# A Silu one place later and two block-sum steps one stage earlier in a two-layer encoder kernel

## The chip, the cores and the metric

The kernel runs on one core of a Trainium2 chip. A core has a matrix engine (TensorE, in the profile PE, with its weight loads as PEld), three engines for elementwise work (VectorE: DVE, ScalarE: ACT, GpSimd: POOL), and queues that start DMA transfers (SP and POOL here). Each engine works through its own instruction queue in order and waits on semaphores for the others. The metric is the device time of one execution in microseconds.

## What is computed

The reference is an encoder of two layers over 512 tokens of width 1024. Both layers end in the same kind of channel mixer, and that is where the change lies:

```python
def conv_ffn(h, w_up, conv_w, conv_b, w_down):
    u, g = jnp.split(h @ w_up, 2, axis=-1)
    g = causal_dwconv(g, conv_w, conv_b)
    return (jax.nn.silu(g) * u) @ w_down
...
x = x + jnp.concatenate([mix_out, mem_out], axis=-1) @ w_out
x = x + conv_ffn(rmsnorm(x, norm_ffn_g[l]), ffn_w_up[l], ffn_conv_w[l], ffn_conv_b[l], ffn_w_down[l])
```

`w_up` has 2 x 2816 columns (up and gate), the convolution runs over three tokens, and `w_down` leads back to 1024. Ahead of the mixer the first layer has a matrix-memory head and a memory attention, the second a banded attention and a memory attention, each with an output projection (`w_out`). All is float32.

## The kernel before

Everything is held transposed: 128 channels on the partitions, 512 tokens along a row. A float32 factor is split into a high and a low part, and each product is three matmuls (high x high, high x low, low x high; `mm3`, lines 194 to 198). The split of a tile is a cast on ACT for the high part and a subtraction on DVE for the low part (`split`, lines 142 and 143).

**Out projection** (`OutProjection.finish`, line 710). For each of the eight x tiles it adds the projection to the residual on DVE (line 715), writes the tile to `xspill` through POOL's queue (716), squares it on ACT and adds the square on DVE for the norm (`Norm.add`, lines 284 to 291), and scales it by the gain into a high part on ACT and a low part on DVE (`scaled`, lines 331 and 332): these are the activations of the mixer. In the first layer it takes, behind x tiles 4, 5 and 6, one step each of `block_sums`.

**Block sums** (`block_sums`, line 781). Step k takes x tiles k and k + 4: two scaled copies on ACT (787), four subtractions of half tiles on DVE (796), and the split of the four results (four casts on ACT, four subtractions on DVE). It has four steps and they are a generator: whoever calls `next` on it has one step emitted at that place.

**Plain tiles** (`plain`, line 759). The mixer has 22 tiles of 128 hidden channels. The first three (PLAIN = 3) are computed plainly: gate and up projection of 24 matmuls each, the gate times the norm's row (770), the convolution's first product on ACT (750) and two taps on DVE (743), Silu on ACT (774), times the row (775), times up (778), split. The norm's row itself is made inside plain tile 0 (`Norm.finish`, line 293): a split of the sum of squares, two matmuls with ones (301), then Ln, Exp and Square on ACT and three products on DVE. The block-sum steps that are still left are woven into the plain tiles, one for each eight products. In the second layer all four steps are left: two fall into plain tile 1, two into plain tile 2.

**Later tiles** (`later` and `step`, lines 850 and 874). The other 19 tiles use a scheme that multiplies blocks of 256 tokens with seven products in place of eight; it needs sums of weight blocks (class `Forms`) and the block sums. One step computes one tile: on TensorE the chain on r1 (889 to 891: product, then ACT's copy to `up`), the chain on r2 (893; added on DVE in 894), the third chain, again on r1 (895; copied by ACT in line 882), the fourth on r3 (897), the fifth on r1 (900; copied by 882), products of the down projection with hidden tiles that are done (904, 911), a sixth on r1 (910), a seventh on r3 (912). r1 is one PSUM bank: its next chain can't start before the last copy out of it is done. The down products go through `add` (line 820): a copy on ACT (822) into a `bias` tile and an accumulating DMA through POOL (823).

What follows the products of a tile, its **tail** (class `Tail`), runs in the next tile's step: the last block's add (989), times the norm's row (992, 995), first tap on ACT (750), two taps on DVE (743), Silu on ACT (1007), the gate product on DVE (1010) and the split of the hidden tile. The weight sums and splits of the tile after it (`nxt`) run in the same step.

**What sets the order.** In `later` all instructions of TensorE, ACT and DVE stand in the order in which `step` emits them (`manual_schedule`, line 862). Outside of it a planner orders each engine's queue at compile time: it takes, of what is ready by its own estimate of costs, what comes first in the program. Tiles of one tag (`u` for splits, `t` for temporaries, `bias`) share a fixed number of buffers, and PSUM has three `mm`, three `sc` and two `tr` banks.

Of the kernel before, what the change touches and what calls it, by code (L numbers as in the profile page):

```python
# [19 lines left out]
KT = D // P  # L20
# [23 lines left out]
LOADS = [(0, 2, 0, 4), (0, 2, 4, 8)]  # L44
LOADS += [(2, 4, 2 * i, 2 * i + 2) for i in range(4)]
LOADS += [(4 * g, 4 * g + 4, 2 * i, 2 * i + 2) for g in (1, 2, 3) for i in range(4)]
UNITS = {3 + i: tuple((i, j) for j in range(*LOADS[i][2:])) for i in range(len(LOADS))}

H = S // 2
# [7 lines left out]
def trunk(  # L57
# [34 lines left out]
    def sb(tag, shape, dtype=F32):  # L92
        count[0] += 1
        return pool.tile(shape, dtype, tag=tag, name=f"{tag}{count[0]}", bufs=bufs[tag])

    def ps(tag):
        count[0] += 1
        return psum.tile([P, S], F32, tag=tag, name=f"p{tag}{count[0]}", bufs=pbufs[tag])
# [101 lines left out]
    def project(w, c0, act, tag="mm"):  # L200


        n = len(act)
        wh, wl = weights(rows(w, c0, P), n, P)
        o = ps(tag)
        for k in range(n):
            mm3(o, wh[:, k, :], wl[:, k, :], act[k][0], act[k][1], k == 0, k == n - 1)
            yield
        return o

    def run(gen):
        while True:
            try:
                next(gen)
            except StopIteration as end:
                return end.value
# [57 lines left out]
    def logarithms():  # L274

        pin(A.preload_act_table_set("natural_log_exp_and_others"))

    class Norm:
# [14 lines left out]
        def finish(self):  # L293


            parts = [sb("t", [P, S], F32R) for _ in range(2)]
            split(*parts, self.acc)
            yield 7.4
            o = ps("sc")
            for i, part in enumerate(parts):  # L300
                nc.tensor.matmul(o, onesr, part, start=i == 0, stop=i == 1)
            v, r, t = sb("rb", [P, S]), sb("t", [P, S]), sb("t", [P, S])
            A.activation(t, o, AF.Ln, scale=1.0 / D, bias=eps)
            V.tensor_scalar(v, o, 1.0 / D, EPS, op0=ALU.mult, op1=ALU.add)
            A.activation(r, t, AF.Exp, scale=-0.5)
            A.activation(t, r, AF.Square)
            yield 4
            V.scalar_tensor_tensor(t, t, -0.5, v, op0=ALU.mult, op1=ALU.mult)
            self.row = sb("rb", [P, S])
            V.scalar_tensor_tensor(self.row, t, 1.5, r, op0=ALU.add, op1=ALU.mult)  # L310
# [18 lines left out]
    def scaled(t, g):  # L329
        hi, lo = sb("u", [P, S], F32R), sb("u", [P, S], F32R)  # L330
        A.activation(hi, t, AF.Copy, scale=g)
        V.scalar_tensor_tensor(lo, t, g, f(hi), op0=ALU.mult, op1=ALU.subtract)  # L332
        return hi, lo
# [131 lines left out]
    with tc.manual_schedule(engines={mybir.EngineType.PE, mybir.EngineType.Activation, mybir.EngineType.DVE}):  # L465
# [20 lines left out]
        def step(products, os_, k, order):  # L486
            for a, b in order:
                for i, o in enumerate(os_):
                    c = slice(i * P, (i + 1) * P)
                    st, mv = kv[k][a], memT[k][b]  # L490
                    first, last = (k, (a, b)) == (0, order[0]), (k, (a, b)) == (KT - 1, order[-1])
                    if products == "keys":
                        nc.tensor.matmul(o, st[:, c], mv, start=first, stop=last)
                    else:
                        nc.tensor.matmul(o, mv[:, c], st[:, MEM:], start=first, stop=last)
# [194 lines left out]
    class OutProjection:  # L690
# [6 lines left out]
        def part(self, g, *ks):  # L697
            j0, j1, tag = self.groups[g]
            if j0 not in self.o:
                self.o.update((j, ps(tag)) for j in range(j0, j1))  # L700
            cols = slice(j0 * P, j1 * P)
            wh, wl = weights([self.w[k * P : (k + 1) * P, cols] for k in ks], len(ks), (j1 - j0) * P)
            for i, k in enumerate(ks):
                self.n[g] += 1
                for j in range(j0, j1):
                    c = slice((j - j0) * P, (j - j0 + 1) * P)
                    mm3(self.o[j], wh[:, i, c], wl[:, i, c], *self.mixes[k], self.n[g] == 1, self.n[g] == KT)
                    yield

        def finish(self, mixer):  # L710
            logarithms()
            norm = mixer.norm
            for j in range(KT):
                o = self.o[j] if j in self.o else run(project(self.w, j * P, self.mixes))
                V.tensor_add(xT[j], xT[j], o)
                pin(G.dma_start(xspill[j], xT[j]))
                norm.add(xT[j])
                mixer.act.append(scaled(xT[j], mixer.gain[:, j : j + 1]))
                if mixer.l == 0 and KT // 2 <= j < KT - 1:
                    next(mixer.forms)  # L720

    class ChannelMixer:
# [127 lines left out]
        def later(self):  # L850


            prep, tail = Forms(self, PLAIN), None
            prep.split_up()
            prep.sums()
            prep.split_second()
            prep.sum_third()
            prep.split_sums()
            prep.sum_fourth()
            prep.split_down()  # L860
            prep.split_gate()
            with tc.manual_schedule(
                engines={mybir.EngineType.PE, mybir.EngineType.Activation, mybir.EngineType.DVE}
            ):
                for j in range(PLAIN, FT):
                    self.beside()
                    tail, prep = self.step(j, prep, Forms(self, j + 1) if j + 1 < FT else None, tail)
            for part in (
                tail.last_block, tail.scaled, tail.first_tap, tail.scaled_up,
                tail.second_tap, tail.third_tap, tail.gated, tail.split,  # L870
            ):
                part()

        def step(self, j, w, nxt, tail):
            def then(o, *names):
                for name in names if o is not None else ():
                    getattr(o, name)()

            def sum_products(o, r, w, i):

                self.products(r, w, self.t(i))
                A.copy(o, r[:, :H])  # L882

            new = Tail(self, j)
            then(tail, "last_block", "scaled")
            w.split_fourth()
            then(tail, "scaled_up")
            r1, r2, new.r3 = ps("mm"), ps("mm"), ps("sc")
            new.up, new.u3, new.pre = sb("t", [P, S]), sb("t", [P, S]), sb("t", [P, S])
            self.products(r1, w.a11, self.b(0, 0), True)  # L890
            A.copy(new.up[:, :H], r1[:, :H])  # L891
            then(tail, "first_tap", "second_tap", "third_tap")
            self.products(r2, w.a12, self.b(1, 0), True)
            V.tensor_tensor(out=new.up[:, :H], in0=new.up[:, :H], in1=r2[:, :H], op=ALU.add)
            sum_products(new.up[:, H:], r1, w.s2, 2)
            then(nxt, "sums")
            self.products(new.r3, w.s1, self.t(1), True)
            then(tail, "gated")
            then(nxt, "split_second", "sum_third")
            sum_products(new.u3[:, :H], r1, w.s3, 3)  # L900
            then(tail, "split")
            then(nxt, "split_up")
            V.tensor_tensor(out=new.pre[:, H:], in0=new.u3[:, :H], in1=new.r3[:, :H], op=ALU.add)
            w.down_products(0, 2)
            then(nxt, "split_sums", "sum_fourth")
            w.add_down(0)
            then(nxt, "split_gate")
            w.add_down(1)
            then(nxt, "split_down")
            sum_products(new.pre[:, :H], r1, w.a22, 4)  # L910
            w.down_products(2, 4)
            self.products(new.r3, w.s4, self.b(1, 1))
            w.add_down(2)
            w.add_down(3)
            return new, nxt

    class Forms:


        def __init__(self, mixer, j):  # L920
            self.mixer = mixer
            self.units = UNITS.get(j, ())
            self.up, self.gate = mixer.load_pair(j)
# [57 lines left out]
    class Tail:  # L981
# [22 lines left out]

        def third_tap(self):
            next(self.taps)
            A.activation(self.acc, self.acc, AF.Silu)

        def gated(self):
# [313 lines left out]
    mixer = ChannelMixer(0, col["gffn"][:, 0:8], more_rows)  # L1323
# [138 lines left out]
    mixer = ChannelMixer(1, col["gffn"][:, 8:16], lambda: None)  # L1462
# [125 lines left out]
```

## Time and profile before

| What | Value |
|---|---|
| median of 3 runs | 1193.42 us (1190.77 to 1195.13) |
| the profiled execution | 1192.76 us |
| its span, first to last instruction | 1191.0 us |
| mean granted clock of TensorE | 0.996 |
| busy: PE, DVE, ACT, POOL | 1171.5, 986.8, 743.1, 143.0 us |
| channel mixer steps, layer 0 and layer 1 (first to last tail Silu) | 329.6 to 585.5 us, 893.2 to 1151.2 us |

A row of the profile's groups names the line, engine and operation, the tile written and those read, the shapes and the count; behind the bar stand busy time, mean duration in ns, and idle time of the engine just before, with what ended it. A row of the timeline gives start, duration, engine, line, operation, tiles, and in brackets idle time before it and what ended it. A row of the waits gives who waited for whom: total us, times, longest. A matmul's duration covers its way through the array, and matmuls overlap: their pitch is the distance of their starts.

### The profile page before, as it was taken

To read this page: it belongs to the slowest core of one execution; us is meant where nothing else is said; L and a number is where in the kernel's file an instruction comes from. 1 tells how busy PE (TensorE), PEld (TensorE's weight loads), DVE (VectorE), ACT (ScalarE), POOL (GpSimd) and SP (SyncE) were. 2 spreads that over 40 slices of the span, in tenths; PEclk is the share of its full clock that TensorE was granted. 3 is DMA by queue.
4 is the path that set the end of the run, shared out by engine and by line. 5 is a ranking of instruction groups with operands and counts; after the bars stand their busy time and mean duration, and the time that the engine had idled before them with its cause. 6 is when DMAs were issued, how large, how long until landed. Compare 5 with 4: busy or idle time off the path is not lost.

```text
span 1191.0 us, 19097 instructions
## 1 busy us (share of the span) xinstructions
PE 1171.5 (98%) x7149; PEld 1040.0 (87%) x7149; DVE 986.8 (83%) x1768; ACT 743.1 (62%) x1345; POOL 143.0 (12%) x238
## 2 busy tenths in 40 slices
PE   9999999999999999999999999999989999999997
PEld 9988888887899999999888888778878999999986
DVE  6776788789889988888788888987878998888865
ACT  6548677657566655555666666776755665555545
POOL 1211101010122111111020001101011111111100
PEclk9999999999999999999999999999989999999999
DMA  8645325244578766665662323236256766666551
GB/s 278 223 110 146 78 54 150 84 145 114 130 166 193 178 165 165 142 141 116 180 212 81 87 70 108 82 113 203 86 121 114 167 143 142 142 141 143 124 159 72
DMA packets 200623, 162.87 MB, mean 137 GB/s; under 512 B 8680, under 2 KB 176334, under 8 KB 200530
## 3 DMA queue, kind: packets, MB, share of 16 engines
q1 hardware_dynamic: 182066, 119.74, 34.3%
q0 software_dynamic: 17888, 40.86, 18.2%
q8 instruction: 56, 0.92, 0.3%
q10 hardware_dynamic: 576, 1.05, 0.2%
q14 instruction: 37, 0.30, 0.1%
HBM read 128.89 MB, written 36.66 MB: 139 GB/s over the span
## 4 chain that ended last, share of the span: by engine, by line
PE 74%; issue 14%; DVE 7%; ACT 3%; POOL 1%; DMA 1%; POOLq 0%; ACTq 0%; DVEq 0%
PE pmm L196 15%; PE pmm L197 14%; PE pmm L198 14%; PE ptr L197 5%; PE ptr L198 5%; PE ptr L196 5%; PE psc L198 3%; PE psc L196 3%; PE psc L197 3%; PE psc L602 2%; DVE wl L143 1%; DVE t L743 1%; ACT wh L142 1%; DVE fl L143 1%; PE ptr L1410 1%
## 5 line engine op out<-in xcount | busy, mean ns | idle before, releaser
L196 PE MATMUL pmm<-u,wh 128*128 128x512 f32 (+1 forms) x984 | 335.8, 342 | 2.9 <-ACT t L882 2.0
L197 PE MATMUL pmm<-u,wh 128*128 128x512 f32 (+1 forms) x984 | 331.9, 337 | 0.2 <-DVE u L332 0.2
L198 PE MATMUL pmm<-u,wl 128*128 128x512 f32 (+1 forms) x984 | 332.0, 338 | 0.0
L143 DVE TENSOR_TENSOR wl<-wr,wh 128x1024 fp32r<-128x1024 f32 (+4 forms) x172 | 195.6, 1138 | 81.8 <-ACT wh L142 81.4
L142 ACT CAST wh<-wr 128x1024 fp32r<-128x1024 f32 (+4 forms) x172 | 168.3, 981 | 81.9 <-PE pmm L197 31.6
L196 PEld LDWEIGHTS pmm<-u,wh 128*128 128x128 f32 x984 | 185.2, 188 | 22.1 <-ACT t L882 4.9
L198 PEld LDWEIGHTS pmm<-u,wl 128*128 128x128 f32 x984 | 185.0, 188 | 19.7 <-DVE wl L143 0.3
L197 PEld LDWEIGHTS pmm<-u,wh 128*128 128x128 f32 x984 | 185.2, 188 | 17.3 <-DVE u L332 0.5
L823 POOL DMA_DIRECT2D xspill<-bias x80 | 69.4, 884 | 428.9 <-ACT bias L822 402.9
L196 PE MATMUL ptr<-u,wh 128*128 128x512 f32 x272 | 106.4, 391 | 0.0
L197 PE MATMUL ptr<-u,wh 128*128 128x512 f32 x272 | 106.3, 391 | 0.0
L198 PE MATMUL ptr<-u,wl 128*128 128x512 f32 x272 | 105.9, 389 | 0.0
L196 PE MATMUL pmm<-u,fh 128*128 128x256 f32 x304 | 85.2, 280 | 6.3 <-ACT t L891 6.3
L142 ACT CAST fh<-pt 128x512 fp32r<-128x512 f32 x114 | 71.2, 625 | 27.2 <-DVE pt L940 26.5
L143 DVE TENSOR_TENSOR fl<-pt,fh 128x512 fp32r<-128x512 f32 x114 | 78.3, 688 | 8.4 <-ACT fh L142 5.5
L197 PE MATMUL pmm<-u,fh 128*128 128x256 f32 x304 | 84.7, 279 | 0.0
L198 PE MATMUL pmm<-u,fl 128*128 128x256 f32 x304 | 84.6, 278 | 0.0
L743 DVE SCALAR_TENSOR_TENSOR t<-t,cols,t 128x511 f32<-128x511 f32 x88 | 66.0, 750 | 10.4 <-ACT t L750 9.0
L822 ACT COPY bias<-ptr 128x512 f32<-128x512 f32 x80 | 46.9, 589 | 39.9 <-PE ptr L198 35.5
L196 PE MATMUL psc<-u,wh 128*128 128x256 f32 (+1 forms) x216 | 67.9, 314 | 0.3 <-ACT wh L142 0.3
L198 PE MATMUL psc<-u,wl 128*128 128x256 f32 (+1 forms) x216 | 67.6, 313 | 0.4 <-DVE wl L143 0.4
L197 PE MATMUL psc<-u,wh 128*128 128x256 f32 (+1 forms) x216 | 67.5, 313 | 0.0
(348 smaller groups left out, 2584.4 us busy)
## 6 DMA issues: line engine op xcount, KB each, us to landing
wr<-in_ffn_w_up_dram SPq DMA_DIRECT2D x50, 512.0 KB, 7.2
xspill<-bias POOLq DMA_DIRECT2D x80, 256.0 KB, 5.7
pt<-in_ffn_w_up_dram SPq DMA_DIRECT2D x38, 512.0 KB, 7.9
wr<-in_ffn_w_down_dram SPq DMA_DIRECT2D x34, 512.0 KB, 5.3
wr<-in_a_w_in_dram SPq DMA_DIRECT2D x20, 512.0 KB, 3.9
wr<-in_w_kv_dram SPq DMA_DIRECT2D x12, 512.0 KB, 4.0
xspill<-fh POOLq DMA_DIRECT2D x16, 256.0 KB, 2.6
xspill<-fl POOLq DMA_DIRECT2D x16, 256.0 KB, 2.7
```

What stands on the lines that cost most here:

```text
L142: high = A.copy(hi, src) if on_act else V.tensor_copy(hi, src)
L143: low = V.tensor_tensor(out=lo, in0=src, in1=f(hi), op=ALU.subtract)
L196: nc.tensor.matmul(o, lh, rh, start=first, stop=False, skip_group_check=more)
L197: nc.tensor.matmul(o, lh, rl, start=False, stop=False, skip_group_check=more)
L198: nc.tensor.matmul(o, ll, rh, start=False, stop=last, skip_group_check=more)
L602: nc.tensor.matmul(o, a, b, start=first and i == 0, stop=i == 1)
L743: V.scalar_tensor_tensor(acc[:, n:], src[:, : S - n], self.fw[:, c * FT + j : c * FT + j + 1], acc[:, n:], op0=ALU.mult, op1=ALU.add,)
L822: A.copy(t, o)
L823: G.dma_start(xspill[j], t, accum_op=ALU.add)
L1410: nc.tensor.transpose(tp[:, b * P : (b + 1) * P], es[T, h][:, b * P : (b + 1) * P], ident)
```

## The change

Two edits. The tail's Silu becomes a part of its own, and `step` calls it behind the third chain's copy instead of right behind the second tap on DVE. A table EARLY says behind which x tile how many block-sum steps are taken: in the first layer one each behind tiles 4, 5 and 7 (before: 4, 5, 6), in the second two behind tile 7 (before: none). The number of plain tiles, three, is the same before and after.

```diff
+EARLY = ({4: 1, 5: 1, 7: 1}, {7: 2})
...
                 pin(G.dma_start(xspill[j], xT[j]))
                 norm.add(xT[j])
                 mixer.act.append(scaled(xT[j], mixer.gain[:, j : j + 1]))
-                if mixer.l == 0 and KT // 2 <= j < KT - 1:
+                for _ in range(EARLY[mixer.l].get(j, 0)):
                     next(mixer.forms)
...
                 tail.last_block, tail.scaled, tail.first_tap, tail.scaled_up,
-                tail.second_tap, tail.third_tap, tail.gated, tail.split,
+                tail.second_tap, tail.third_tap, tail.silu, tail.gated, tail.split,
...
             self.products(r2, w.a12, self.b(1, 0), True)
             V.tensor_tensor(out=new.up[:, :H], in0=new.up[:, :H], in1=r2[:, :H], op=ALU.add)
             sum_products(new.up[:, H:], r1, w.s2, 2)
+            then(tail, "silu")
             then(nxt, "sums")
             self.products(new.r3, w.s1, self.t(1), True)
             then(tail, "gated")
...
         def third_tap(self):
             next(self.taps)
+
+        def silu(self):
             A.activation(self.acc, self.acc, AF.Silu)
```

## Prediction

> **What bounds the kernel now.** I read the page first, then the waits of the matmul engine's weight loads, then the timeline around the longest of those waits, and last the windows of single stages.
>
> ```profile
> span 1191.0 us, 19097 instructions
> PE 1171.5 (98%) x7149; PEld 1040.0 (87%) x7149; DVE 986.8 (83%) x1768; ACT 743.1 (62%) x1345; POOL 143.0 (12%) x238
> PEclk9999999999999999999999999999989999999999
> ```
>
> TensorE is busy for 98% of the span, so only what makes TensorE wait, or slows its clock, can be won. The clock row has one digit that is not 9, slice 29 (863 to 893 us): in one place TensorE ran slower. The execution took 1192.76 us, 1.8 us more than its span; the three timed runs have a median of 1193.42.
>
> ```profile
> PEld pmm L196 <- ACT t L891: 6.9, 3, 4.5
> PEld pmm L196 <- ACT t L882: 5.6, 13, 0.9
> L196 PEld LDWEIGHTS pmm<-u,wh 128*128 128x128 f32 x984 | 185.2, 188 | 22.1 <-ACT t L882 4.9 <-ACT u L142 1.0
> L196 PEld LDWEIGHTS pmm<-u,fh 128*128 128x128 f32 x304 | 57.6, 189 | 9.0 <-ACT t L891 6.9 <-ACT t L882 0.7
> ```
>
> These are the waits on the two copies out of r1's PSUM bank: L891, after a step's first chain, and L882, after its third to fifth. Both concern the steps of the later tiles, and both edits aim at them. Of the thirteen waits on L882 two (0.7 us, the `fh` group) belong to the last step of each layer and are not touched; the other eleven, 4.9 us, are fifth chains waiting for the third chain's copy.
>
> **Edit 1, the Silu.** One short step of layer 0 shows the cause (ACT, PE and DVE rows of the timeline):
>
> ```profile
> 357.42 0.63 ACT L1007 ACTIVATE t<-t 128x512 f32<-128x512 f32 x1 [1.89 <-DVE t L743]
> 357.95 0.35 ACT L882 COPY t<-pmm 128x256 f32<-128x256 f32 x1
> 356.60 0.28 PE L198 MATMUL pmm<-u,fl 128*128 128x256 f32 x1
> 357.96 0.28 PE L198 MATMUL psc<-u,wl 128*128 128x256 f32 x1
> 358.36 0.38 PE L196 MATMUL pmm<-u,wh 128*128 128x256 f32 x1
> 358.90 0.69 DVE L1010 TENSOR_TENSOR t<-t,t 128x512 f32<-128x512 f32 x1
> ```
>
> The third chain ends at 356.60 + 0.28 = 356.88, but its copy starts at 357.95: it stands behind the Silu, for which ACT waited 1.89 us on the second tap. The fourth chain's last matmul starts at 357.96; the fifth, on the same bank, could start a pitch (0.11) later and starts 0.40 later. With the copy ahead it runs from 356.9 to 357.3 inside ACT's 1.89 us of waiting, the Silu still starts at 357.42, and the gate product L1010, queued on DVE behind the block-sum adds of the next tile, sees no difference. Nothing else moves: the edit adds and removes no instruction, no DMA, no tile.
>
> The price, summed: 4.9 us of idle loads, and each wait costs 0.08 more than its idle time, because a load takes 0.19 (188 ns in the group's row) and the pitch is 0.11. 4.9 + 11 x 0.08 = **5.7 us**.
>
> What is late next in such a step? DVE.
>
> ```profile
> 349.24:361.90 12.66, 12.54 (x98) 11.85 (x96) 12.25 (x19) 8.39 (x16) 2.98 (x4) 1.00 0.69 170
> 411.00:426.00 15.00, 15.00 (x110) 14.04 (x110) 13.00 (x20) 8.78 (x15) 2.92 (x4) 1.00 0.70 169
> ```
>
> In these windows (columns: length, then busy time and count of PE, PEld, DVE, ACT, POOL, then clock and DMA) the short step has 12.25 us of DVE work in 12.66, so it can shrink by 0.41, just the 0.40 at stake; the rest of its loop shrinks too, since DVE's own wait comes from a weight cast that follows the fifth chain. Cover is there, but none to spare. The long step (15.0 us) has no stall and 2 us of idle DVE. There taps and third chain end together, so the Silu becomes about 0.2 to 0.3 later:
>
> ```profile
> 410.72 0.28 PE L198 MATMUL pmm<-u,fl 128*128 128x256 f32 x1
> 411.06 0.63 ACT L1007 ACTIVATE t<-t 128x512 f32<-128x512 f32 x1 [1.66 <-DVE t L743]
> 412.54 0.69 DVE L1010 TENSOR_TENSOR t<-t,t 128x512 f32<-128x512 f32 x1
> ```
>
> Copy from 411.0 to 411.3, Silu to 411.9, gate product at 412.54 as before: 0.6 us to spare. Cost nothing; were it not so, 2 us of idle DVE per long step would take it.
>
> **Edit 2, the block sums.** A step is two ACT copies, four DVE subtractions and four splits (a cast on ACT, a subtraction on DVE each), with no DMA; SP and POOL see it only through the buffers that DVE frees. Its DVE pitch:
>
> ```profile
> 863.16 0.42 DVE L796 TENSOR_TENSOR t<-u 128x256 f32<-128x256 f32 x1
> 863.50 0.42 DVE L796 TENSOR_TENSOR t<-u,u 128x256 f32<-128x256 f32 x1
> ```
>
> 0.34 x 8 = 2.7 us a step. In layer 1 two steps move from behind plain tile 1's seventh and later products to behind x tile 7; the two left then fall into tile 1, and tile 2 has none. The wait this concerns:
>
> ```profile
> 866.98 0.28 PE L198 MATMUL pmm<-u,wl 128*128 128x256 f32 x1
> 868.88 0.74 DVE L743 SCALAR_TENSOR_TENSOR t<-t,cols,t 128x510 f32<-128x510 f32 x1
> 869.72 0.63 ACT L774 ACTIVATE t<-t 128x512 f32<-128x512 f32 x1 [0.32 <-DVE t L743]
> 870.25 1.00 ACT L142 CAST u<-t 128x256 fp32r<-128x256 f32 x3
> 871.16 0.36 ACT L891 COPY t<-pmm 128x256 f32<-128x256 f32 x1
> 871.57 0.58 PE L196 MATMUL pmm<-u,fh 128*128 128x256 f32 x1 [4.32 <-ACT t L891]
> 867.20:870.70 3.50, 0.06 (x1) 0.00 (x0) 3.50 (x8) 2.45 (x6) 0.00 (x0) 1.00 0.39 110
> 871.50:877.50 6.00, 5.93 (x27) 5.93 (x28) 5.24 (x12) 1.63 (x4) 0.00 (x0) 0.50 0.31 87
> 831.40:868.90 37.50, 35.86 (x170) 29.94 (x169) 33.08 (x58) 27.17 (x44) 0.54 (x1) 1.00 0.31 93
> ```
>
> TensorE stands from 867.1 to 871.57 (4.5 us) for a copy that is queued on ACT behind plain tile 2's Silu and three casts of the fourth block-sum step. The clock is 1.00 through the first 3.5 us of that pause and 0.50 for the 6 us after it, which costs another 3.0 us. All this is because DVE is late: from x tile 7's add (831.4) to the second tap (868.88) it has 33.1 us of work and 4.4 idle.
>
> Ledger of that stretch afterwards. Before the second tap, 3 steps and one subtraction of the fourth ran (8 + 0.3 us); then all four will: +2.4. The idle time by cause:
>
> ```profile
> DVE wl L143 <- ACT wh L142: 1.8, 3, 1.3
> DVE t L743 <- ACT t L750: 0.9, 1, 0.9
> DVE rb L291 <- ACT t L290: 0.7, 1, 0.7
> DVE pt L940 <- DMA wr<-in_ffn_w_up_dram: 0.5, 1, 0.5
> ```
>
> The waits on weight casts (1.8) and on a load (0.5) go, because the moved steps give DVE work meanwhile; the other two stay, 1.6. The second tap then starts at 831.4 + 33.1 + 2.4 + 1.6 = 868.5, 0.4 earlier, and the three casts (870.25 to 871.16, 0.9) no longer stand ahead of the copy. The copy gains 1.3, the pause falls to 3.2 us, and as 3.5 us of pause passed at full clock, the 3.0 of half clock go. Sum **4.3 us**. Bounds: if all 4.4 of idle stay, the tap is 2.0 later and the pause grows by 1.1 (-1.1); if the planner, which orders all outside the hand-ordered part by its own costs, puts the copy ahead of the Silu, pause and half clock go whole (+7.5). I stay near the middle, at the ledger. What follows is DMA-bound: the next step's L891 waits for a spill to land, a chain that starts at an ACT copy behind TensorE's fifth chain and so moves with it.
>
> The cover of the moved steps: PSUM holds three gate and three up tiles, so TensorE runs through all plain tiles without the norm row. It needs weights, though:
>
> ```profile
> 834.20 0.69 DVE L143 TENSOR_TENSOR t<-rb,t 128x512 fp32r<-128x512 f32 x1
> 836.00 0.63 PE L301 MATMUL psc<-t,onesr 128*128 128x512 f32 x2
> 836.16 1.23 DVE L143 TENSOR_TENSOR wl<-wr,wh 128x1024 fp32r<-128x1024 f32 x1 [1.27 <-ACT wh L142]
> 842.61 0.39 PE L196 MATMUL pmm<-u,wh 128*128 128x512 f32 x1
> ```
>
> Behind 5.4 us of moved work, the low half for tile 1's gate is ready at 836.2 + 5.4 + 1.2 = 842.8, when TensorE reaches it (842.6): 0.2 at most. Who waits on the two steps: the norm's split (834.20) and all that hangs on its row.
>
> In layer 0 the third step goes from behind x tile 6 to behind 7. DVE was working without a pause there, and the same work lies before the same taps. TensorE had two stops nearby:
>
> ```profile
> 280.92 0.50 PE L197 MATMUL pmm<-u,wh 128*128 128x512 f32 x1 [0.16 <-DVE u L332]
> 282.05 0.50 PE L198 MATMUL psc<-u,wl 128*128 128x512 f32 x1 [0.40 <-DVE wl L143]
> ```
>
> They may go (+0.6), or the norm row comes a step later (-2.7). I take 0, the first being nearer.
>
> **Sum**: 1192.8 - 5.7 - 4.3 = 1182.8 for the profiled execution, whose time is 0.7 below the median; against the median **1183.4**.
>
> **Rivals** (times against the median). *The pause whole*: the copy is planned ahead of the Silu; 1193.4 - 5.7 - 7.5 = 1180.2. For it: the planner places L891 by its own estimate, and the change shifts that. Against: before, it placed it last. Chance 0.18.
>
> *The pause stays*: DVE keeps over 2 us of its idle, the pause passes 3.5 us and the half clock stays; about 0.5 gained, 1187.2. For it: two steps now stand ahead of the norm's row, whose chain through ACT and DVE cannot overlap with itself. Chance 0.17.
>
> *The half clock is not in the typical run*: the pause is 4.5 us and the drop came about 3.5 us into it; if the drop depends on when the pause falls, the median run lost no 3.0 us here, and only 5.7 + 1.3 are won: 1186.4. The trace has one such pause, which dropped, and no pause of 1.2 us did. [...] Chance 0.15.
>
> *DVE binds the short steps*: the 0.41 of idle DVE is latency that stays in part, and half of edit 1 is lost: 1193.4 - 2.9 - 4.3 = 1186.2. Chance 0.08.
>
> *The norm row is late and everything with it (slower)*: TensorE's ones-matmul at 836.00 keeps its place in the queue and waits for the split, which now stands behind two steps (5.4) in layer 1 and behind a whole one (2.7) in layer 0. If none is absorbed: 1193.4 + 8.1 - 5.7 = 1195.8. It decides from about 6 us of unabsorbed delay on. Against it: 1.1 us of slack in layer 1 (834.89 to 836.00), and that the planner may put other products ahead of a matmul whose input is late. Chance 0.06.
>
> **How the numbers follow.** The forecast has 0.36. A measurement of this kernel can tell about 0.5%, 6.0 us, from no change: faster is below 1187.4. Nearly all of the forecast's chance, all of 1180.2's, half of 1187.2's and about two thirds of 1186.4's and 1186.2's lie there: 0.76. Slower is the last rival less its small outcomes: 0.05; 0.19 remain. The range goes from 1178.5 (the whole pause, 0.6 in layer 0, and some of the scatter of the runs, 1190.77 to 1195.13) to 1190.0 (the pause grown by 1.1 with the half clock kept, 1188.8, and layer 0 losing some).
>
> **What would show it.** Edit 1 is right if the waits on L882 fall from 13 to about 2, short steps take 12.3 us instead of 12.7, and the Silu's own start and the gate product keep their distance; wrong if DVE shows no idle in a 12.5 us step. Edit 2 is right if the pause before step 3's third chain in layer 1 is some 3 us and the clock row is all nines; wrong if L796 stands in the DVE queue ahead of a late ones-matmul with TensorE idle beside it. The forecast as a whole is wrong if the stages outside both channel mixers change.

## The result, and the profile after

| Kernel | median | runs | ratio to before, 95% interval |
|---|---|---|---|
| before | 1192.93 us | 4 (1190.77 to 1195.13) | |
| changed | 1186.56 us | 4 (1184.86 to 1187.14) | 0.9944 [0.9923, 0.9966] |

The change made the kernel 6.4 us faster. The forecast was 1183.4 and its range held the result, but the sum behind it is not what happened: one of its two edits gave all of the gain and a little more than was forecast for it, the other gave nothing. The profiled execution of the changed kernel took 1186.16 us. From here on lines of the kernel are those of the changed one: 142 and 143 have become 143 and 144, 882 is 883, 891 is 892, 822 and 823 are 823 and 824, 301 is 302, 743 is 744, 774 is 775, 1007 is 1011 and 1010 is 1014.

The page, span, engines and the granted clock:

```profile
span 1184.4 us, 19103 instructions
PE 1166.5 (98%) x7149; PEld 1037.1 (88%) x7149; DVE 984.5 (83%) x1768; ACT 744.1 (63%) x1345; POOL 143.3 (12%) x238
PEclk9999999999999999999999999999999999999999
```

The one digit that was not 9 has become a 9. That looks like the forecast's second edit at work; further down it turns out to be something else. The waits of TensorE's weight loads (total us, times, longest):

```profile
PEld pmm L197 <- ACT wh L143: 4.0, 2, 2.7
PEld pmm L197 <- ACT t L892: 3.9, 3, 2.2
PEld pmm L199 <- DVE wl L144: 2.4, 2, 1.4
...
PEld pmm L197 <- ACT t L883: 0.7, 2, 0.4
```

The waits on L883, the copy behind which the Silu went, fell from 13 to 2, the two of the last steps. The waits on L892 fell from 6.9 to 3.9. But two rows are new: 6.4 us of waits for the high and low parts of weights (L143, L144), of which before had none of this size.

A short step of layer 0, third chain to third chain, of before and of the changed kernel (columns as in the prediction), and the changed kernel's ACT and DVE rows in the timeline:

```profile
349.91:362.58 12.67, 12.55 (x98) 11.86 (x97) 12.26 (x20) 8.40 (x16) 3.40 (x5) 1.00 0.71 173
349.31:361.58 12.27, 12.27 (x98) 11.78 (x96) 12.11 (x20) 8.52 (x16) 3.57 (x5) 1.00 0.75 179
```

```profile
356.31 0.37 ACT L883 COPY t<-pmm 128x256 f32<-128x256 f32 x1 [1.40 <-PE pmm L199]
356.81 0.63 ACT L1011 ACTIVATE t<-t 128x512 f32<-128x512 f32 x1
358.29 0.68 DVE L1014 TENSOR_TENSOR t<-t,t 128x512 f32<-128x512 f32 x1
```

TensorE is busy for the whole of the step. The copy now waits for TensorE and not for the Silu; from the Silu's start to the gate product it is 1.48 us, as before (357.42 to 358.90).

The plain stage of layer 1 (timeline, ACT, DVE and PE):

```profile
833.61 0.39 PE L199 MATMUL pmm<-u,wl 128*128 128x512 f32 x1
...
835.15 1.03 ACT L143 CAST wh<-wr 128x1024 fp32r<-128x1024 f32 x1
...
836.08 1.08 ACT L143 CAST u<-t 128x256 fp32r<-128x256 f32 x3
836.23 0.50 PE L197 MATMUL pmm<-u,wh 128*128 128x512 f32 x1 [2.23 <-ACT wh L143]
...
837.06 0.62 ACT L143 CAST t<-rb 128x512 fp32r<-128x512 f32 x1
...
837.96 0.40 PE L302 MATMUL psc<-t,onesr 128*128 128x512 f32 x1
838.20 0.40 PE L197 MATMUL psc<-u,wh 128*128 128x512 f32 x1
```

Here is where the second edit went. `pmm` is a gate tile, `psc` an up tile or the norm's ones-matmul (`onesr`). TensorE ends the products it has at 833.6 + 0.4 and stands 2.23 us until the weights of a later plain tile's gate have been cast. Meanwhile not one product of plain tile 0's up projection has run. They come at 838.20, all behind the ones-matmul, which waits for the norm's split (`t<-rb`, 837.06), and that now stands behind the casts of the moved block sums (836.08). Something keeps the up products behind the ones-matmul.

What each stage won or lost shows in the starts of the same product in the two traces:

| Product | before | changed | lead |
|---|---|---|---|
| one of layer 0's out projection | 251.03 | 250.04 | 1.0 |
| first of the third chain, layer 0's first later step | 312.50 | 312.32 | 0.2 |
| first of the sixth chain, layer 0's last step | 579.72 | 576.82 | 2.9 |
| first of the third chain, layer 1's first later step | 871.57 | 868.31 | 3.3 |
| first of the sixth chain, layer 1's last step | 1145.68 | 1139.08 | 6.6 |

Most of the first lead comes from the kernel's start, where TensorE ran slowly for longer in before: six matmuls of 256 tokens lead up to 7.31 us of the span there at a mean pitch of 0.22 us (first start 5.96), and up to 6.32 us in the changed kernel at one of 0.15 (first start 5.42); the pitch of those behind them is 0.12 in both. Layer 0's plain stage then lost 0.8. The short steps of the two layers gave 2.7 and 3.0 us, and a wait on the third chain's copy in layer 1's step 4 (894.18 in before) about 0.5; together 6.2.

The rest, 0.4, is small because large parts cancel. In layer 1 before's pause of 4.3 us is won, and some 2.7 of the half clock around its end: the granted clock is 0.50 from 870.77 to 877.60, and TensorE worked through 6.0 us of that stretch, at a pitch of 0.213 us for matmuls of 256 tokens, where 0.118 or less is the pitch at full clock. Lost are the stop of 2.23, another of 1.24 at the low weights of the first later tile (865.70), 1.3 more than before in two stops on L892, and some 1.5 in a half-clock stretch of 3.41 us (0.50 from 886.29 to 889.70) behind the first of them. These parts sum to 0.7, and the starts leave 0.2 of it; the difference is about the pitch lost beside each stop's idle time (behind the stop of 2.23 us the first two products are 0.34 us apart and the next ones 0.23).

### The profile page after: what moved, and what is told of

It is laid out like the page before. It is cut to its first block, busy times and chain, and to the rows that moved or that the text cites. A ratio compares the mean times of both kernels' runs of the same rounds, so it can differ in the third digit from the quotient of the medians.

```text
span 1184.4 us, 19103 instructions
## 1 busy us (share of the span) xinstructions
PE 1166.5 (98%) x7149; PEld 1037.1 (88%) x7149; DVE 984.5 (83%) x1768; ACT 744.1 (63%) x1345; POOL 143.3 (12%) x238
## 4 chain that ended last, share of the span: by engine, by line
PE 82%; issue 12%; DVE 2%; ACT 1%; POOL 1%; DMA 1%; POOLq 0%; ACTq 0%; DVEq 0%
PE pmm L197 16%; PE pmm L198 16%; PE pmm L199 16%; PE ptr L198 6%; PE ptr L197 5%; PE ptr L199 5%; PE psc L198 4%; PE psc L197 4%; PE psc L199 4%; PE psc L603 2%; PE ptr L1414 1%; DVE wl L144 1%; DMA xspill<-bias 1%; PE ptr L1435 0%; PE ptr L1436 0%
## 5 line engine op out<-in xcount | busy, mean ns | idle before, releaser
L144 DVE TENSOR_TENSOR wl<-wr,wh 128x1024 fp32r<-128x1024 f32 (+4 forms) x172 | 195.7, 1138 | 74.0 <-ACT wh L143 73.4
L143 ACT CAST wh<-wr 128x1024 fp32r<-128x1024 f32 (+4 forms) x172 | 168.3, 981 | 81.4 <-PE pmm L198 32.7
L143 ACT CAST fh<-pt 128x512 fp32r<-128x512 f32 x114 | 71.0, 625 | 32.7 <-DVE pt L942 32.3
L883 ACT COPY t<-pmm 128x256 f32<-128x256 f32 x114 | 42.7, 375 | 71.1 <-PE pmm L199 70.9
L144 DVE TENSOR_TENSOR fl<-pt,fh 128x512 fp32r<-128x512 f32 x114 | 78.3, 688 | 9.6 <-ACT fh L143 6.7
L823 ACT COPY bias<-ptr 128x512 f32<-128x512 f32 x80 | 46.8, 588 | 40.2 <-PE ptr L199 34.7
L197 PE MATMUL psc<-u,wh 128*128 128x256 f32 (+1 forms) x216 | 67.6, 313 | 0.0
```

The lines of the kernel that those rows point to most:

```text
L143: high = A.copy(hi, src) if on_act else V.tensor_copy(hi, src)
L144: low = V.tensor_tensor(out=lo, in0=src, in1=f(hi), op=ALU.subtract)
L197: nc.tensor.matmul(o, lh, rh, start=first, stop=False, skip_group_check=more)
L823: A.copy(t, o)
```

## The experiments

Twelve kernels, each timed in rounds beside the kernel before. Its median was 1192.29, 1192.12 and 1190.97 us in the three groups of runs, so runs of different groups are compared by their ratio; 0.001 is 1.2 us.

| Run | Silu | block sums | ones-matmul's bank | bias tiles | us | ratio, 95% interval |
|---|---|---|---|---|---|---|
| changed | moved | moved | sc | ahead | 1186.56 | 0.9944 [0.9923, 0.9966] |
| e1 | moved | before | sc | ahead | 1186.11 | 0.9946 [0.9932, 0.9960] |
| e2 | before | moved | sc | ahead | 1192.82 | 1.0004 [0.9995, 1.0013] |
| e3 | moved | layer 1 moved | sc | ahead | 1185.80 | 0.9944 [0.9932, 0.9956] |
| e5 | moved | moved | tr | ahead | 1181.79 | 0.9913 [0.9900, 0.9927] |
| e8 | moved | before | tr | ahead | 1186.71 | 0.9952 [0.9939, 0.9964] |
| e10 | moved | moved | sc, behind up's | ahead | 1182.15 | 0.9920 [0.9907, 0.9932] |
| e6 | moved | moved | sc | later | 1182.34 | 0.9916 [0.9902, 0.9929] |
| e7 | moved | moved | tr | later | 1176.90 | 0.9875 [0.9859, 0.9890] |
| e9 | moved | three early in layer 1 | tr | later | 1177.93 | 0.9878 [0.9865, 0.9892] |
| e11 | moved | before | tr | later | 1182.18 | 0.9925 [0.9912, 0.9937] |
| e12 | moved | layer 1 moved | tr | later | 1179.03 | 0.9898 [0.9882, 0.9913] |
| e13 | before | moved | tr | later | 1181.79 | 0.9925 [0.9913, 0.9937] |

**Each edit alone.** e1 is the changed kernel with the table of steps as it was:

```diff
-EARLY = ({4: 1, 5: 1, 7: 1}, {7: 2})
+EARLY = ({4: 1, 5: 1, 6: 1}, {})
```

> Edit 1 alone: the Silu behind the third chain's copy, the block sums as before (layer 0 behind x tiles 4, 5, 6; layer 1 none early). Theory A (the gain is edit 1's; edit 2 only breaks one long stop of TensorE into shorter ones and gives back as much as it saves): 6.3 us faster than the kernel before, about 1186.5, the same as the changed kernel within 1 us; the 4.5 us pause ahead of layer 1's first step is still there, the waits on L882 are gone. Theory B (edit 2 carries part of it, by the shorter pause and the clock that holds): only 2 to 4 us faster, 1189 to 1191.

e2 is the changed kernel with the Silu where it was:

```diff
-            then(tail, "first_tap", "second_tap", "third_tap")
+            then(tail, "first_tap", "second_tap", "third_tap", "silu")
...
-            then(tail, "silu")
```

> Edit 2 alone: the block sums as in the changed kernel, the Silu right behind the second tap as before. Theory A: no difference, -0.5 to +1 us against the kernel before, with the eleven waits on the third chain's copy all there. Theory B: 2.5 to 4.5 us faster, 1188.5 to 1190.5.

e3 has the Silu moved and layer 1's two steps, but not layer 0's:

```diff
-EARLY = ({4: 1, 5: 1, 7: 1}, {7: 2})
+EARLY = ({4: 1, 5: 1, 6: 1}, {7: 2})
```

> The changed kernel with layer 0's third step back behind x tile 6; layer 1 keeps its two early steps. Theory A: the stops of 1.1 and 0.7 us at layer 0's first plain tile go back to the 0.4 and 0.6 of before, 0.8 us faster than the changed kernel (1185.8). Theory B (the step behind tile 7 lets the norm's row start sooner): 0.5 us slower than the changed kernel.

Measured: 1186.11, 1192.82 and 1185.80. The Silu alone gives 6.2 us, the whole gain; the block sums alone give nothing, within 0.0013 either way. e3's ratio is the changed kernel's; layer 0's step is too small to be seen in medians here. So the question became why the moved steps give nothing, though e1 still has the whole pause that they should have shortened:

```profile
868.48 0.38 PE L197 MATMUL pmm<-u,fh 128*128 128x256 f32 x1 [4.31 <-ACT t L892]
```

**The bank of the ones-matmul.** In the program the norm's ones-matmul takes an `sc` bank (`o = ps("sc")`) ahead of plain tile 0's up projection, whose tiles have `sc` banks too. If banks of one kind are given out in the program's order, no up product can be planned ahead of the ones-matmul. e5 gives it a bank of another kind:

```diff
-            o = ps("sc")
+            o = ps("tr")
```

> The changed kernel with the norm's ones-matmul in a bank of the tag tr in place of sc. Theory A (in the changed kernel the planner can't start plain tile 0's up projection before the ones-matmul, because its sc bank is given out behind the norm's; it fills in products whose weights aren't cast yet, and TensorE stops 2.2 us for them): that stop goes, up products stand ahead of the ones-matmul; but VectorE is as late as before, so most comes back as a stop ahead of the first step: 0 to 1 us faster than the changed kernel (1185.5 to 1186.5). Theory B (the stop is the moved steps' own load on ScalarE): the stop stays at 2 us and the time is that of the changed kernel.

Measured: 1181.79. It gained 0.0031, or 3.7 us, on the changed kernel, where 0 to 1 had been expected. The stop of 2.23 us is gone, which the moved steps' own load on ScalarE (the expectation's theory B) can't explain. The timeline of PE and ACT at the same place:

```profile
831.16 0.39 PE L199 MATMUL pmm<-u,wl 128*128 128x512 f32 x1
...
831.39 0.39 PE L197 MATMUL psc<-u,wh 128*128 128x512 f32 x1
...
834.61 0.62 ACT L143 CAST t<-rb 128x512 fp32r<-128x512 f32 x1
...
835.28 0.50 PE L302 MATMUL ptr<-t,onesr 128*128 128x512 f32 x1
```

The up products start one pitch after the gate's, and the norm's split (`t<-rb`) is made beside them. Is that the bank alone, or the bank together with the moved steps? e8 is e5 with the steps where they were before:

```diff
-EARLY = ({4: 1, 5: 1, 7: 1}, {7: 2})
+EARLY = ({4: 1, 5: 1, 6: 1}, {})
```

> The norm's ones-matmul in the other bank (as in the run that did only this to the changed kernel, 1181.79), and the block sums where they were before the change (layer 0 behind x tiles 4, 5, 6; none early in layer 1). Theory 'masked': moving the block sums is worth 1 to 3 us once the ones-matmul no longer holds back the next up product, so without the move this is 1183 to 1185. Rival 'bank alone': the gain of the other bank does not depend on where the block sums stand: within 0.5 us of 1181.8.

Measured: 1186.71, the time of e1. Without the move the bank is worth nothing (e1 to e8); without the bank the move is worth nothing (e1 to the changed kernel, and e2). With the bank the move is worth 0.0039, 4.6 us (e8 to e5); both together, against e1 which has neither, are worth 0.0033, 3.9 us. My theory had called the move masked and was right in sign, but sized it at 1 to 3.

Is it the kind of bank, or only the order in which banks are given out? e10 keeps the `sc` bank and emits two more products ahead of the norm, so that the up tile's bank is taken first:

```diff
-            yield 7.4
+            yield 9.4
```

> The changed kernel; the norm's ones-matmul keeps its bank of the sc kind, but plain tile 0's up projection is given its own bank first (two more products are emitted ahead of the norm in the program). Theory 'order of the banks': what holds TensorE is that the up products can't be planned ahead of a ones-matmul whose bank of the same kind was given out earlier; with the up bank first they can, and this runs as the kernel with the ones-matmul in a tr bank: 1181 to 1183 (changed kernel 1186.56). Rival 'the kind of bank': it is the tr bank itself that helps, by leaving all three sc banks to the up tiles, and here nothing is won: 1186 to 1187.

Measured: 1182.15, ratio 0.9920; e5's was 0.9913 and the changed kernel's 0.9944. So the order does it. Its timeline has the same sequence as e5's, with the ones-matmul in `psc`:

```profile
831.26 0.39 PE L199 MATMUL pmm<-u,wl 128*128 128x512 f32 x1
831.48 0.39 PE L197 MATMUL psc<-u,wh 128*128 128x512 f32 x1
...
835.37 0.50 PE L302 MATMUL psc<-t,onesr 128*128 128x512 f32 x1
835.71 0.40 PE L199 MATMUL psc<-u,wl 128*128 128x512 f32 x1
```

**The stops behind it.** The changed kernel has two more stops in layer 1's first steps, 2.05 us at 886.05 and 1.23 us at 904.21, both for L892. They are not new, only longer: before stood at the same two places (timeline, PE):

```profile
890.69 0.38 PE L196 MATMUL pmm<-u,fh 128*128 128x256 f32 x1 [1.00 <-ACT t L891]
907.84 0.39 PE L196 MATMUL pmm<-u,fh 128*128 128x256 f32 x1 [1.02 <-ACT t L891]
```

The changed kernel's timeline ahead of the first (ACT):

```profile
884.62 0.59 ACT L823 COPY bias<-ptr 128x512 f32<-128x512 f32 x1 [2.84 <-DMA xspill<-bias]
885.10 0.62 ACT L143 CAST fh<-pt 128x512 fp32r<-128x512 f32 x1
...
885.62 0.38 ACT L892 COPY t<-pmm 128x256 f32<-128x256 f32 x1
```

The down product's copy (L823) waits 2.84 us for the transfer that frees a `bias` tile, and the copy for which TensorE stands is queued on ACT behind it. Of the four `bias` tiles two are taken ahead of layer 1's channel mixer for the final gain, which is used only after it. e6 allots them later:

```diff
-    fgb = [sb("bias", [P, S]) for _ in range(2)]
-    for hf in range(2):
-        G.dma_start(fgb[hf], ...)
...
     hid = channel_mixer(mixer)
+    fgb = [sb("bias", [P, S]) for _ in range(2)]
+    for hf in range(2):
+        G.dma_start(fgb[hf], ...)
```

> The changed kernel, with the two bias tiles that take the final gain (and their loads) allotted behind layer 1's channel mixer instead of ahead of it, so that its down products have four such tiles and not two. Theory 'bias tiles': in the first steps of layer 1 the down product's copy waits for a spill to land and free a bias tile (2.84 us in front of one such copy), stands in ACT's queue ahead of the next copy to up, and TensorE stops for 2.05 and 1.23 us and then runs 3.4 us at half clock: 3.3 of stops, and 1.7 for the half clock, go. 3.8 to 5.3 us faster than the changed kernel's 1186.56: 1181.3 to 1182.8. Rival 'order on ACT': the copies come late by ACT's own order and the spill only fills the time: the stops stay, and the time is within 1 us of 1186.56.

Measured: 1182.34. Both stops are gone; e6's waits have no row for L892 among the largest:

```profile
PEld pmm L197 <- ACT wh L143: 4.0, 2, 2.6
PEld pmm L199 <- DVE wl L144: 2.4, 2, 1.4
PEld ptr L1414 <- DVE pt L144: 1.2, 4, 0.4
```

The theory of the bias tiles holds: no copy on ACT waits for a spill in e6's mixer steps. The half clock that was to go with the stops does not show as won: the mean granted clock of e6's profiled execution is 0.998, as in the changed kernel's. The weights' rows of the changed kernel are left, as the ones-matmul still has its bank. e7 joins the two (e5's and e6's edits):

> The changed kernel with the ones-matmul in the other bank and the bias tiles allotted later. Theory 'two separate losses': the bank gave 4.8 us and the bias tiles give about 4, the stops of 1.53 and 2.85 us that are left in the first run with the other bank go: 1176.5 to 1178.5. Rival 'order on ACT': the stops stay, 1181 to 1182.

Measured: 1176.90, 0.9875. The two gains add: 0.0031 and 0.0028 from the changed kernel make 0.0059, and 0.0069 was measured, the same within the uncertainty of some 0.002. e7 is the best kernel of the study, 15.2 us ahead of the one before (1192.12 in this group). One pause of 2.1 us is left in it ahead of step 3's third chain:

```profile
PEld pmm L197 <- ACT t L892: 2.3, 1, 2.3
PEld ptr L1414 <- DVE pt L144: 1.2, 4, 0.4
```

**The edits again, where nothing stands in their way.** e11, e12 and e13 undo parts of the change in e7: e11 all block sums, e12 those of layer 0, e13 the Silu.

```diff
-EARLY = ({4: 1, 5: 1, 7: 1}, {7: 2})
+EARLY = ({4: 1, 5: 1, 6: 1}, {})
```

> The run with other bank and later bias tiles (1176.9), with all block sums where they were before the change. Theory 'the move is worth 5 once the bank does not block it' (1186.71 against 1181.79 with the bias tiles ahead): 5 slower, 1181 to 1183. Rival 'the difference of 5 was in the spill waits that the move shifts': with those waits gone the move is worth under 2: 1177 to 1179.

```diff
-EARLY = ({4: 1, 5: 1, 7: 1}, {7: 2})
+EARLY = ({4: 1, 5: 1, 6: 1}, {7: 2})
```

> The same run (1176.9) with only layer 0's third step back behind x tile 6. From the stops in layer 0 that the move takes away there (0.17, 0.41 and 0.50 us of idle, and what each costs beside): 1 to 2.7 slower, 1178 to 1179.6. Rival, the forecast's term of 0 for layer 0: 1176.5 to 1177.3.

```diff
-            then(tail, "first_tap", "second_tap", "third_tap")
+            then(tail, "first_tap", "second_tap", "third_tap", "silu")
...
-            then(tail, "silu")
```

> The same run (1176.9) with the tail's Silu back behind the second tap, the block sums as in the changed kernel. If the Silu's gain lies in the short steps alone and is the same whatever the plain stage does: 6.0 to 6.6 slower, 1183 to 1183.5. Rival: part of what it gained was shifted waits of the first steps of layer 1: 4.5 to 5.5 slower.

Measured against e7's 0.9875: e11 0.9925, e12 0.9898, e13 0.9925. In e7 the whole move is worth 0.0050 (6.0 us), layer 0's part of it 0.0023 (2.7), the Silu 0.0050 (6.0). Each difference is uncertain by about 0.002. The traces are finer: the Silu's part is 5.0 us by the spans (1179.7 and 1174.7). e13's trace has nine waits on the third chain's copy beside those of the last steps, 3.7 us, where before had eleven, 4.9 us; so it is nearer the rival, that part of the gain lay in waits of layer 1's first steps, but the medians don't decide. Between e12 and e7 layer 0's first later step starts its third chain at 311.45 and 309.26, 2.2 earlier; 0.3 of that is there at layer 0's out projection already (the same product starts at 250.06 and 249.79). e12 still has three stops there (timeline, PE), e7 none:

```profile
279.98 0.50 PE L198 MATMUL pmm<-u,wh 128*128 128x512 f32 x1 [0.17 <-DVE u L333]
281.11 0.50 PE L199 MATMUL psc<-u,wl 128*128 128x512 f32 x1 [0.40 <-DVE wl L144]
298.27 0.50 PE L197 MATMUL psc<-u,wh 128*128 128x512 f32 x1 [0.27 <-ACT wh L143]
```

Layer 1's part is the difference of e11 and e12, here the second tap, the Silu, the casts and the copy of e11 (timeline, ACT, DVE and PE):

```profile
865.30 0.74 DVE L744 SCALAR_TENSOR_TENSOR t<-t,cols,t 128x510 f32<-128x510 f32 x1
...
866.14 0.63 ACT L775 ACTIVATE t<-t 128x512 f32<-128x512 f32 x1 [0.32 <-DVE t L744]
...
866.67 1.00 ACT L143 CAST u<-t 128x256 fp32r<-128x256 f32 x3
...
867.58 0.36 ACT L892 COPY t<-pmm 128x256 f32<-128x256 f32 x1
...
867.99 0.58 PE L197 MATMUL pmm<-u,fh 128*128 128x256 f32 x1 [4.31 <-ACT t L892]
```

and of e12:

```profile
864.09 0.62 ACT L143 CAST u<-t 128x512 fp32r<-128x512 f32 x1 [1.40 <-DVE t L779]
864.69 0.81 ACT L751 ACTIVATE t<-t,cols 128x512 f32<-128x512 f32 x1
865.41 0.35 ACT L892 COPY t<-pmm 128x256 f32<-128x256 f32 x1
...
865.81 0.52 PE L197 MATMUL pmm<-u,fh 128*128 128x256 f32 x1 [2.09 <-ACT t L892]
...
868.10 0.74 DVE L744 SCALAR_TENSOR_TENSOR t<-t,cols,t 128x510 f32<-128x510 f32 x1
...
868.99 0.64 ACT L775 ACTIVATE t<-t 128x512 f32<-128x512 f32 x1
```

The pause falls from 4.31 to 2.09, 2.2 us, and TensorE reaches it at the same time in both (its last product ahead of it starts at 863.4). In e11 plain tile 2's Silu (866.14) and the casts stand ahead of the copy; in e12 its second tap is 2.8 us later (868.10 against 865.30) and the planner has put the copy ahead of the Silu, behind the first product of that tile's convolution (L751) and a cast that waits 1.40 for DVE. With three steps early in layer 1 (e9) even this pause goes:

```diff
-EARLY = ({4: 1, 5: 1, 7: 1}, {7: 2})
+EARLY = ({4: 1, 5: 1, 7: 1}, {4: 1, 5: 1, 7: 1})
```

> Bank and bias tiles as in the run with both, and in layer 1 three block-sum steps early (behind x tiles 4, 5 and 7, as layer 0 has them) in place of two behind x tile 7. The theory of the forecast, that the copy ahead of step 3's third chain is late because DVE has block sums ahead of the second tap: the pause of about 2 us there becomes under 1, 1 to 2 us faster than the run with both. Rival: DVE has the same work before that tap wherever the steps stand, so the pause and the time stay within 0.6 us.

Measured: 1177.93 against e7's 1176.90, no difference by the intervals, where 1 to 2 us less had been expected. The pause has gone, as the first theory said, but it is paid elsewhere. Its timeline has a stop of the same size among the first gate products, as the weights' subtraction now stands behind an early step's work on DVE:

```profile
825.18 0.50 PE L199 MATMUL pmm<-u,wl 128*128 128x512 f32 x1 [2.12 <-DVE wl L144]
```

## Why the forecast was near, and where its sum failed

**What bounds the kernel** was read rightly: TensorE's stops and its half clock are the whole account.

**Edit 1** was forecast at 5.7 and gave 6.2 (e1), and 5 to 6 in the freed kernel (e13). Every step of it held: the waits on the copy fell from 13 to 2, a short step from 12.67 to 12.27 us, the Silu and the gate product kept their distance. DVE had 12.26 us in that step before and 12.11 after, so the little cover there was (0.41) was enough, and the rival *DVE binds the short steps* falls.

**Edit 2, the cover.** The step that failed is the sentence "PSUM holds three gate and three up tiles, so TensorE runs through all plain tiles without the norm row". The number of tiles was right; but the norm's ones-matmul takes one of the same `sc` banks, and takes it first in the program. With it late, plain tile 0's up products, whose weights are there, are late with it, and TensorE goes on to gates whose weights are not. The forecast allowed 0.2 us for a gate's weights; the stops were 2.23 and, at the low weights of the first later tile, 1.24 us. e5, e8 and e10 show it: the same moved steps give some 4 us once the up tile's bank is given out apart or first (0.0039 from e8 to e5, 0.0032 from e8 to e10). This is the mechanism of the rival that ended on the slower side (*the norm row is late*), which had named the ones-matmul's place in the queue but priced it at 8.1 and thought that other products could go ahead of it. The price paid was some 3.5 us in layer 1 and 0.8 in layer 0, and with the longer stops on L892 that followed and their half clock it used up all that the pause and its half clock had cost.

**Edit 2, the pause.** The forecast had it fall from 4.5 to 3.2 us in layer 1. In the changed kernel the pause is gone, but because TensorE arrives late (its last product ahead of that chain starts at 868.20; before's did at 866.98, with layer 0 ending 2.9 us later), not because the copy is early; the copy still stands behind the Silu (867.28, then 867.82). This, and no early copy, took the dip out of the clock row; a shorter one 15 us later doesn't show in its tenths. In the freed kernel the move takes 2.2 us from it, not 1.3. The ledger itself is wrong there: it had the second tap 0.4 us earlier and the copy behind it. In e12 the tap is 2.8 us later, past the ledger's own bound of 2.0, and the copy comes 2.2 earlier all the same, because the planner put it ahead of the Silu. That is the mechanism of the rival *the pause whole*; but not the whole pause goes, since the copy has other work ahead of it.

**Edit 2, the half clock.** The 3.0 us were counted as won if the pause stays under 3.5 us. The size was near (some 2.7 by the pitch); the bound is wrong. A pause of 2.08 us was followed by half clock in e5 and by none in e7 (the last section). *The half clock is not in the typical run* asked whether a pause like before's can pass without it; none did: all four pauses of 4.31 to 4.57 us in the timelines (before, e1, e8, e11) had half clock behind them. How much of it came behind one pause length differed: 27 matmuls ran at half clock behind before's pause of 4.32 us and 15 behind e11's of 4.31. What sets that is not shown.

**What follows.** That the chain "so moves with it" failed as well. With the plain stage changed, the two stops behind the transfers that free the `bias` tiles did not stay at 1.00 and 1.02 us but became 2.05 and 1.23; e6, which gives the mixer four tiles, has neither.

**Layer 0** was taken at 0 between +0.6 and -2.7. As built it lost 0.8, inside; freed, its third step is worth about 2 us, outside, because the stops took more than their idle time: with the pitch lost around each of them (0.34 us behind each in e12, where 0.23 is the usual), 0.84 us of idle made up some 1.8 of loss.

So of the forecast's 10.0 us, 5.7 came as 6.2 and 4.3 as nothing. That the time fell inside the range was its width and not its sum: with edit 2 at nothing the forecast would have been 1187.7, which the range from 1178.5 to 1190.0 held too. The rivals at 1187.2 and 1186.4 were near by their numbers and not by their mechanisms. What stays open: whether the last pause, 2.1 us in e7, would go if the copy were put ahead of that first product and cast too; no run took only that away.

## What to carry to other kernels

When a step is moved ahead of something small, such as a sum's matmul, look not only at who waits for that result but at who waits for its buffer: what is given out in the program's order stands in line behind it, though its own data are there. And a move that measures nothing need not be worth nothing: here one line elsewhere (the bank) was worth nothing alone, the move nothing alone, and both together some 4 us. A stop that is removed can hand time to the next in line: in e5, without the weights' stops, the two stops on L892 were 1.53 and 2.85 us, against 2.05 and 1.23 in the changed kernel. Only all four (Silu, block sums, bank, bias tiles) together gave 15 us.

## What the hardware showed

Between the kernel's start and its last 3 us the granted clock of before is 0.50 in one stretch of 6.83 us (870.77 to 877.60) and that of the changed kernel in one of 3.41 us (886.29 to 889.70). In the other runs half clock shows as matmuls of 256 tokens at a pitch of 0.213 us in place of 0.118 (of 512 tokens in e9, 0.43 in place of 0.23). What followed TensorE's pauses in the timelines (the idle time before the product that ended the pause):

| Pause | half clock behind it | full clock behind it |
|---|---|---|
| 1.00 to 1.24 us | none | before (1.00 and 1.02), changed (1.24 and 1.23), e6 (1.22), e8 (1.20), e10 (1.23) |
| 2.05 to 2.12 us | changed (2.05), e5 (2.08), e10 and e12 (2.09), e9 (2.12) | e7 (2.08), e13 (2.09) |
| 2.23 to 2.85 us | none | changed (2.23), e1 (2.50), e2 and e5 (2.85) |
| 4.31 to 4.57 us | e1 and e11 (4.31), before (4.32), e8 (4.57) | none |

e5 and e7 have the same pause of 2.08 us; here the 3.41 us with the pause and those after them, of e5 (columns as above: length, PE, PEld, DVE, ACT, POOL, clock, DMA share, GB/s):

```profile
861.81:865.22 3.41, 1.33 (x12) 1.13 (x11) 3.41 (x6) 1.67 (x3) 0.00 (x0) 1.00 0.00 0
865.22:868.64 3.42, 3.42 (x19) 3.42 (x18) 3.42 (x6) 1.00 (x2) 0.00 (x0) 0.50 0.16 47
```

and of e7:

```profile
861.93:865.34 3.41, 1.58 (x14) 1.59 (x14) 3.41 (x6) 1.67 (x3) 0.00 (x0) 1.00 0.00 0
865.34:868.75 3.41, 3.41 (x29) 3.28 (x28) 3.41 (x6) 1.00 (x2) 0.00 (x0) 1.00 0.38 106
```

Behind the pause e5 ran at 0.50, 19 matmuls in 3.42 us (those that only overlap its ends counted too), and e7 at 1.00, 29 matmuls in 3.41. In e5 the first product behind the pause starts at 864.24, and the half clock 1.0 us later. Of the five kernels with a pause of 2.08 or 2.09 us three (e5, e10, e12) had half clock after it and two (e7, e13) had not, and four longer ones, of 2.23 to 2.85 us (changed, e1, e2, e5), had none. So the length of a pause alone did not decide it between 2.05 and 2.85 us, and what did is not shown. The half clock cost a little less than half its length: in e5's stretch the pitch of matmuls of 256 tokens is 0.213 us and behind it 0.118, which makes some 1.5 us of 3.42. The scatter between the changed kernel's runs goes with the clock: its four took 1184.86, 1186.16, 1186.95 and 1187.14 us at mean granted clocks of 0.999, 0.998, 0.998 and 0.997. For a pause of some 2 us, then, the trace of one kernel did not tell what another's would show.
